# The last sums of a stage end quarter by quarter, and the last quarter is transposed between the two halves of the next stage's first weight unit

## The chip, the cores and the metric

The kernel runs on one core of a Trainium2 chip. The metric is the device time of one execution in microseconds, taken as the median of several runs. Five engines work side by side: TensorE (PE; its weight loads are PEld) multiplies and transposes, VectorE (DVE), ScalarE (ACT) and GpSimd (POOL) work element by element, and SyncE (SP) issues the loads and stores.

## What is computed

Two transformer blocks run over one sequence of 256 tokens with 1024 features. The first block has two layers; each adds a mixer to x (a short gated convolution in layer 0, windowed attention in layer 1) and then a PEER layer, in which every token chooses 16 of 16384 experts in each of 8 heads. The second block adds one mixed layer (pooling, mLSTM and blockwise attention side by side) and a gated feed-forward network (FFN). Ahead of every one of these x is normalised:

```python
def _rmsnorm(x, g):
    xf = x.astype(jnp.float32)
    y = xf * lax.rsqrt(jnp.mean(xf * xf, axis=-1, keepdims=True) + RMS_EPS)
    return (y * g.astype(jnp.float32)).astype(x.dtype)
...
    for i in range(DEPTH):
        j = i // N_MIXERS
        if i % N_MIXERS == 0:
            x = x + _short_conv_mixer(_rmsnorm(x, conv_norm_g[j]), conv_w_in[j], conv_w[j], conv_w_out[j])
        else:
            x = x + _windowed_gqa(_rmsnorm(x, attn_norm_g[j]), attn_w_qkv[j], attn_sink[j],
                                  attn_w_o[j], rel_bias)
        x = x + _peer(_rmsnorm(x, ffn_norm_g[i]), peer_w_q[i], peer_subkeys[i], peer_u[i], peer_v[i])
    return _rmsnorm(x, final_norm_g)
```

## The kernel before

All products are made in float32 precision out of three products of halves: a number is split into a high half (a copy to a shorter float) and a low half (what is left), and high x high, high x low and low x high are summed. Weights stream in as units of 128 x 1024. For each unit SyncE loads it into one of four `raw` buffers, ScalarE casts the high half `wh` (L127) into one of three buffers, and VectorE or POOL makes the low half `wl` (L128). `lo_on["pat"]` says which of the two: "P" is POOL, "V" is VectorE. `pump_split` does this up to a unit, `prepare` up to three units ahead of use. The loads that it issues wait for a `raw` buffer, that is, for the low half of the unit four places back.

Two kinds of products use a unit. `c_unit` (weights stand, 24 products of 256 columns, 8 column groups k) gives an output with tokens along the columns. `t_mm` (tokens stand, 12 products of 512 columns) gives an output with tokens along the partitions. The sums at the end of a stage are of the second kind. They fill four PSUM banks 4 to 7, one for each token half b and 512 columns n; such a sum is called a quarter (b, n) here.

At the end of a stage `t_end` takes the last two units together and closes the quarters in turn. `arrive` adds a quarter to x on VectorE (`add_x`, L243 or L245) and transposes its four column groups of x on TensorE (L269) into PSUM, two groups to a bank (`spot`). Then `settle` brings the transposed x, times the gain g, to the two halves that the next stage multiplies with: ScalarE copies a group (L278), VectorE makes its low half (L279). After the first token half it splits one more weight unit, with POOL. The row scales of the norm are not in it: `norm_scales` works them out beside the first unit (sums of squares on ScalarE, a short chain on VectorE), and `spread` lays them along the columns with an identity times the scale (L328), a product with ones (L329) and a copy to `rbc` (L330).

This happens at five places: conv to peer 0 (about 98 to 111 us), peer 0 to attention (927), attention to peer 1 (1031), peer 1 to block 2 (1860; here with `low=True`, where both token halves of a group share a bank, and the first units are of the kind `t_mm`), and block 2's mixer to the FFN (1999). A sixth `t_end` closes the kernel with the stores of the result.

The order on TensorE and SyncE is that of the program text. On ScalarE, VectorE and POOL a scheduler sets a fixed order when the kernel is built: an instruction goes when its inputs are there, the earlier one in the text first. `behind(st["after"])` puts an instruction behind a given one on its engine; `settle` sets it to its last copy, so that the casts and the sums of squares traced later queue behind that.

In `peer`, SyncE loads the subkeys (L421) and stores x to `x_d` (L423) after `settle`; the first scores (L429) need the subkeys. `rescale` (L562 to L565), `top16` and the choice of experts run on VectorE beside the units; the transposes L502 to L504 take what they give.

Of the kernel before, what the change touches and what calls it, by code (L numbers as in the profile page):

```python
# [40 lines left out]
def kernel(ctx: ExitStack, tc: tile.TileContext, a, out):  # L41
# [122 lines left out]

    def t_half(o, h, l, sh, sl, b, n, first, last):
# [38 lines left out]
    def t_end(k, n, get, cur, arrive):  # L204
# [15 lines left out]
        for nn in range(2):  # L220
            arrive(0, nn)
            part(1, nn, 0)
        for nn in range(2):
            part(1, nn, 1)
        for nn in range(2):
            arrive(1, nn)

    def t_phase(n, get, cur, arrive, during=None, k0=0, root=True):
        if root:
            table("sqrt_and_others")  # L230
        pat, lo_on["pat"] = lo_on["pat"], "V"
        t_run(k0, n - 2, n, get, cur, during)
        t_end(n - 2, n, get, cur, arrive)
        lo_on["pat"] = pat
# [30 lines left out]
    def landing(scale=None, low=False):  # L265
        def arrive(b, n):
            add_x(b, n, scale)
            for c in range(4 * n, 4 * n + 4):
                T.transpose(spot(b, c, low), x[:, b, c * 128:c * 128 + 128], ident)  # L269
        return arrive  # L270

    def settle(g, low=False, dst=None):

        h, l = dst or (xh, xl)
        for b in range(2):
            bs = slice(b * 128, b * 128 + 128)
            for c in range(8):
# [3 lines left out]
            if b == 0:  # L281
# [3 lines left out]
        st["after"] = i  # L285
# [39 lines left out]
    def spread(bk, off=0):  # L325

        for b in range(2):
            V.tensor_scalar(gt[b][:, :128], ident, col(b, 5, off), None, op0=ALU.mult)  # L328
            T.matmul(bk[:, b * 128:b * 128 + 128], ones, gt[b][:, :128], start=True, stop=True)  # L329
# [67 lines left out]
    t_phase(8, lambda k: split_small(G[k]), first, landing(), root=False)  # L397


    def peer(layer):  # L400
        xq = renew(F32R)
        xq = [xq[:, 8 * i:8 * i + 8] for i in range(2)]
        settle(cols[:, C_FFNG + 8 * layer:C_FFNG + 8 * layer + 8], dst=xq)
# [174 lines left out]
        lo_on["pat"] = "P"  # L578
        st["ready"] = 0
        for hp in range(18):  # L580
            if hp < 16:
# [3 lines left out]
                c_unit(bank[hp % 3][:, :256], src=xq)  # L585
                if hp == 0:
                    norm_scales()
# [50 lines left out]
        t_phase(128, lambda k: split_small(slot(k)), cur, landing(1.0 / WSCALE, layer == 1), during)  # L638
# [12 lines left out]
    def attention():  # L651
# [11 lines left out]
        settle(cols[:, C_ATTNG:C_ATTNG + 8])  # L663
        lo_on["pat"] = "P"
        for i in range(2):
            c_unit(bank[i][:, :256])
            if i == 0:
                norm_scales()
# [103 lines left out]
        t_phase(8, lambda k: split_small(ao[k]), cur, landing(), None, 4)  # L772
# [21 lines left out]
    def block2():  # L794
        sg = ar(64, 2).rearrange("p (b n) -> p b n", b=2)
        settle(g2, low=True)

        for k in range(8):
# [3 lines left out]
            if k == 0:  # L802
                norm_scales_final(gbc)
# [499 lines left out]
```

## Time and profile before

| | us |
|---|---|
| three runs | 2204.69, 2203.78, 2201.51 |
| median | 2203.78 |
| the profiled execution, its own time | 2201.73 |
| its span, first to last instruction | 2200.0 |

| engine | busy, share of the span |
|---|---|
| TensorE, products and transposes | 97% |
| TensorE, weight loads | 88% |
| VectorE | 76% |
| ScalarE | 52% |
| POOL | 19% |

A busy share is a mean over stages that have different limits. The profile's page gives it for the whole execution; the timeline lists the instructions in order of time with the wait ahead of each and the engine and line that ended it; the windows give the busy time by stretch. A group of equal instructions that follow each other stands in one row with its count; its time is from the first's start to the last's end.

### The profile page before, as it was taken

Reading aid. Unit: us, or ns where it says so; the run is one execution under the profiler, and the core shown is the slowest. Engines: PE = TensorE matmul, PEld = TensorE weight load, DVE = VectorE, ACT = ScalarE, POOL = GpSimd, SP = SyncE. Lnnn points to the kernel's source line nnn. Section 1 sums busy time; section 2 is a strip of 40 time slices with the busy share of each in tenths; the row PEclk is TensorE's granted clock in tenths of the full one; section 3 lists DMA queues with packets and bytes.
Section 4 is the critical chain, followed back from the end, with each engine's and each line's share of the span. In section 5 each row is a group of like instructions: output and inputs, shape, how many; then the busy total and the mean of one; then the engine's idle time right before and its main releaser. Section 6 shows DMA issues by size and latency. Waiting matters only on the chain.

```text
span 2200.0 us, 38262 instructions
## 1 busy us (share of the span) xinstructions
PE 2131.1 (97%) x14590; PEld 1943.2 (88%) x14590; DVE 1675.0 (76%) x3091; ACT 1145.7 (52%) x2102; POOL 409.1 (19%) x176
## 2 busy tenths in 40 slices
PE   9999799999999999998997999999999999889999
PEld 9899799999988888886997999999888888768998
DVE  7799968897566666676999688965666666797998
ACT  4455345554555555566553455545555555655443
POOL 0068630000000000053686300000000001550000
PEclk9999899999999999999998999999999999999999
DMA  7586454445667666633554554456676665434564
GB/s 230 173 238 192 138 176 155 154 155 173 202 194 238 208 192 193 190 116 98 181 168 134 175 157 154 154 173 203 194 223 193 192 193 180 146 94 143 184 189 145
DMA packets 109024, 384.44 MB, mean 175 GB/s; under 512 B 11876, under 2 KB 15332, under 8 KB 108584
## 3 DMA queue, kind: packets, MB, share of 16 engines
q1 hardware_dynamic: 108552, 381.81, 56.1%
q8 instruction: 114, 1.87, 0.3%
q14 instruction: 70, 0.57, 0.1%
q10 hardware_dynamic: 288, 0.19, 0.0%
HBM read 374.61 MB, written 7.34 MB: 174 GB/s over the span
## 4 chain that ended last, share of the span: by engine, by line
PE 88%; DVE 5%; issue 3%; POOL 2%; ACT 1%; DMA 1%; POOLq 0%; SPq 0%; ACTq 0%
PE bank L159 15%; PE bank L161 15%; PE bank L160 15%; PE bank L177 12%; PE bank L178 12%; PE bank L181 12%; PE bank L532 3%; POOL wl L128 2%; DVE arena L857 1%; ACT wh L127 1%; PE bank L429 0%; DMA x_d<-x 0%; PE bank L735 0%; DVE x L243 0%; DVE wl L128 0%
## 5 line engine op out<-in xcount | busy, mean ns | idle before, releaser
L127 ACT ACTIVATE wh<-raw 128x1024 fp32r<-128x1024 f32 x691 | 732.3, 1060 | 466.3 <-PE bank L160 226.9
L128 DVE TENSOR_TENSOR wl<-raw,wh 128x1024 fp32r<-128x1024 f32 x537 | 659.1, 1227 | 256.0 <-ACT wh L127 255.3
L159 PE MATMUL bank<-xh,wh 128*128 128x256 f32 x2792 | 808.9, 290 | 19.0 <-ACT arena L553 11.3
L161 PE MATMUL bank<-xh,wl 128*128 128x256 f32 x2792 | 795.2, 285 | 2.0 <-POOL wl L128 1.4
L160 PE MATMUL bank<-xl,wh 128*128 128x256 f32 x2792 | 794.8, 285 | 0.0
L128 POOL TENSOR_TENSOR wl<-raw,wh 128x1024 fp32r<-128x1024 f32 x154 | 390.4, 2547 | 959.7 <-ACT wh L127 957.7
L159 PEld LDWEIGHTS bank<-xh,wh 128*128 128x128 f32 x2792 | 539.8, 193 | 24.9 <-ACT arena L553 12.1
L161 PEld LDWEIGHTS bank<-xh,wl 128*128 128x128 f32 x2792 | 539.4, 193 | 4.5 <-POOL wl L128 3.2
L160 PEld LDWEIGHTS bank<-xl,wh 128*128 128x128 f32 x2792 | 540.2, 193 | 1.5 <-DVE xl L279 0.8
L177 PE MATMUL bank<-wh,ah 128*128 128x512 f32 x1160 | 454.6, 392 | 0.0
L178 PE MATMUL bank<-wl,ah 128*128 128x512 f32 x1160 | 453.2, 391 | 0.0
L181 PE MATMUL bank<-wh,al 128*128 128x512 f32 x1160 | 358.1, 390 | 0.0
L186 ACT ACTIVATE ah<-arena 128x256 fp32r<-128x256 f32 x270 | 112.3, 416 | 286.9 <-PE bank L178 279.2
L177 PEld LDWEIGHTS bank<-wh,ah 128*128 128x128 f32 x1160 | 218.8, 189 | 47.1 <-issue 2.1
L181 PEld LDWEIGHTS bank<-wh,al 128*128 128x128 f32 x1160 | 218.5, 188 | 45.9
L178 PEld LDWEIGHTS bank<-wl,ah 128*128 128x128 f32 x1160 | 218.8, 189 | 44.5
L187 DVE TENSOR_TENSOR al<-arena,ah 128x256 fp32r<-128x256 f32 x270 | 114.7, 425 | 118.9 <-PE bank L181 109.5
L523 DVE TENSOR_TENSOR x<-iota,ijT 128x1024 f16<-128x1024 f16 x128 | 89.9, 704 | 53.0 <-PE bank L532 53.0
L310 POOL TENSOR_TENSOR top<-x,arena 128x512 f32<-128x512 f32 x4 | 5.1, 1288 | 631.9 <-DVE x L245 631.9
L546 ACT ACTIVATE arena<-bank 128x284 f32<-128x284 f32 (+42 forms) x128 | 38.8, 303 | 131.0 <-DVE arena L544 131.0
L525 DVE TENSOR_TENSOR x<-x,wT 128x1024 f16<-128x1024 f16 x128 | 96.2, 753 | 0.0
L532 PE MATMUL bank<-x 128*128 128x128 f16 x1024 | 81.2, 220 | 0.0
(296 smaller groups left out, 1978.9 us busy)
## 6 DMA issues: line engine op xcount, KB each, us to landing
raw<-in_u_dram SPq DMA_DIRECT2D x256, 512.0 KB, 3.5
raw<-in_v_dram SPq DMA_DIRECT2D x256, 512.0 KB, 3.6
raw<-in_ff_dram SPq DMA_DIRECT2D x66, 512.0 KB, 3.5
raw<-in_wq_dram SPq DMA_DIRECT2D x32, 512.0 KB, 3.6
raw<-in_conv_in_dram SPq DMA_DIRECT2D x23, 512.0 KB, 3.8
raw<-in_conv_out_dram SPq DMA_DIRECT2D x8, 512.0 KB, 3.5
f_d<-arena SPq DMA_DIRECT2D x8, 512.0 KB, 7.1
raw<-in_aq_dram SPq DMA_DIRECT2D x8, 512.0 KB, 3.8
```

The costliest lines, as they stand in the source:

```text
L127: S.activation(h, r, AF.Copy)
L128: (P if pat[lo_on["i"] % len(pat)] == "P" else V).tensor_sub(l, r, h)
L159: T.matmul(out_ps, hv[:, k], ah[:, k], start=k == 0, stop=False)
L160: T.matmul(out_ps, hv[:, k], al[:, k], start=False, stop=False)
L161: T.matmul(out_ps, lv[:, k], ah[:, k], start=False, stop=k == 7)
L177: T.matmul(bank[4 + b * 2 + n], sh[:, bs], h[:, ns], start=first, stop=False)
L178: T.matmul(bank[4 + b * 2 + n], sh[:, bs], l[:, ns], start=False, stop=False)
L181: T.matmul(bank[4 + b * 2 + n], sl[:, bs], h[:, ns], start=False, stop=last)
L186: S.activation(h, src, AF.Copy)
L187: V.tensor_sub(l, src, h)
L525: V.tensor_tensor(W, E[:, 1:2].to_broadcast(shape), wT[:, c, :, :, None, :].to_broadcast(shape), op=ALU.mult)
L532: T.matmul(bk[:, t * 128:t * 128 + 128], E[:, 0, t // 2, :, t % 2], W[:, q, t // 2, :, t % 2], start=q == 0, stop=q == 1)
```

## The change

`t_end` gets two functions in place of `arrive`: `add` adds a quarter to x, `turn` transposes it. The last sums are reordered so that quarter (1,0) is closed before quarter (1,1), and each quarter is added when it is closed. Quarter (0,0) is transposed ahead of token half 1 as before, (0,1) after quarter (1,0) is closed, (1,0) before the last three products. The transposes of (1,1) are kept in `st["turn"]`.

`settle` goes by quarters and takes `first`: it calls `first(0)` after quarter (1,0), then transposes quarter (1,1), copies it, and calls `first(1)`. In four stages `first` is `c_halves`, the first unit in two halves of 12 products with column groups 0 to 3 and 4 to 7; `prepare` runs in its second half. In block 2 `first` is a whole unit each time. `norm_scales` follows `settle`. `spread` makes the two identities times scales with one product on VectorE and one product with ones of 256 columns.

```diff
@@ -162,6 +162,23 @@
         if ahead:
             prepare()
 
+    def c_halves(out_ps, src=None):
+
+        u = []
+
+        def half(i):
+            if not i:
+                u.extend(unit())
+            ah, al = src or (xh, xl)
+            hv, lv = [w.rearrange("p (k m) -> p k m", k=8) for w in u]
+            for k in range(4 * i, 4 * i + 4):
+                T.matmul(out_ps, hv[:, k], ah[:, k], start=k == 0, stop=False)
+                T.matmul(out_ps, hv[:, k], al[:, k], start=False, stop=False)
+                T.matmul(out_ps, lv[:, k], ah[:, k], start=False, stop=k == 7)
+            if i:
+                prepare()
+        return half
+
     def t_half(o, h, l, sh, sl, b, n, first, last):
         bs = slice(b * 128, b * 128 + 128)
         ns = slice(n * 512, n * 512 + 512)
@@ -201,7 +218,7 @@
             if during:
                 during(k)
 
-    def t_end(k, n, get, cur, arrive):
+    def t_end(k, n, get, cur, add, turn=lambda b, n: None):
 
         pat, lo_on["pat"] = lo_on["pat"], "P"
         prepare()
@@ -217,20 +234,24 @@
         for nn in range(2):
             part(0, nn, 0)
             part(0, nn, 1)
-        for nn in range(2):
-            arrive(0, nn)
-            part(1, nn, 0)
-        for nn in range(2):
-            part(1, nn, 1)
-        for nn in range(2):
-            arrive(1, nn)
-
-    def t_phase(n, get, cur, arrive, during=None, k0=0, root=True):
+            add(0, nn)
+        turn(0, 0)
+        part(1, 0, 0)
+        part(1, 0, 1)
+        add(1, 0)
+        turn(0, 1)
+        part(1, 1, 0)
+        turn(1, 0)
+        part(1, 1, 1)
+        add(1, 1)
+        st["turn"] = turn
+
+    def t_phase(n, get, cur, add, turn, during=None, k0=0, root=True):
         if root:
             table("sqrt_and_others")
         pat, lo_on["pat"] = lo_on["pat"], "V"
         t_run(k0, n - 2, n, get, cur, during)
-        t_end(n - 2, n, get, cur, arrive)
+        t_end(n - 2, n, get, cur, add, turn)
         lo_on["pat"] = pat
 
     def sumsq(b, n, src=None, off=0):
@@ -263,26 +284,37 @@
         return bank[i][:, o:o + 128]
 
     def landing(scale=None, low=False):
-        def arrive(b, n):
+        def add(b, n):
             add_x(b, n, scale)
+
+        def turn(b, n):
             for c in range(4 * n, 4 * n + 4):
                 T.transpose(spot(b, c, low), x[:, b, c * 128:c * 128 + 128], ident)
-        return arrive
-
-    def settle(g, low=False, dst=None):
+        return add, turn
+
+    def settle(g, first, low=False, dst=None):
+
 
         h, l = dst or (xh, xl)
-        for b in range(2):
+
+        def quarter(b, n):
             bs = slice(b * 128, b * 128 + 128)
-            for c in range(8):
+            for c in range(4 * n, 4 * n + 4):
                 i = S.activation(h[:, c, bs], spot(b, c, low), AF.Copy, scale=g[:, c:c + 1])
                 V.scalar_tensor_tensor(l[:, c, bs], spot(b, c, low), g[:, c:c + 1], h[:, c, bs],
                                        op0=ALU.mult, op1=ALU.subtract)
-            if b == 0:
+            return i
+
+        for b, n in ((0, 0), (0, 1), (1, 0)):
+            quarter(b, n)
+            if (b, n) == (0, 1):
                 pat, lo_on["pat"] = lo_on["pat"], "P"
                 pump_split(st["use"] + 2)
                 lo_on["pat"] = pat
-        st["after"] = i
+        first(0)
+        st["turn"](1, 1)
+        st["after"] = quarter(1, 1)
+        first(1)
 
     def root(b, off=0):
 
@@ -324,9 +356,9 @@
 
     def spread(bk, off=0):
 
-        for b in range(2):
-            V.tensor_scalar(gt[b][:, :128], ident, col(b, 5, off), None, op0=ALU.mult)
-            T.matmul(bk[:, b * 128:b * 128 + 128], ones, gt[b][:, :128], start=True, stop=True)
+        V.tensor_tensor(gt[0].rearrange("p (b t) -> p b t", b=2), ident[:, None, :].to_broadcast([128, 2, 128]),
+                        sm[:, off + 5:off + 14:8, None].to_broadcast([128, 2, 128]), op=ALU.mult)
+        T.matmul(bk[:, :256], ones, gt[0], start=True, stop=True)
         V.tensor_copy(rbc, bk[:, :256])
 
     def rsqrt_small(dst, v, t):
...
-    t_phase(8, lambda k: split_small(G[k]), first, landing(), root=False)
+    t_phase(8, lambda k: split_small(G[k]), first, *landing(), root=False)
...
-        settle(cols[:, C_FFNG + 8 * layer:C_FFNG + 8 * layer + 8], dst=xq)
+        lo_on["pat"] = "P"
+        settle(cols[:, C_FFNG + 8 * layer:C_FFNG + 8 * layer + 8], c_halves(bank[0][:, :256], xq), dst=xq)
...
-                c_unit(bank[hp % 3][:, :256], src=xq)
-                if hp == 0:
+                if hp:
+                    c_unit(bank[hp % 3][:, :256], src=xq)
+                else:
                     norm_scales()
...
-        settle(cols[:, C_ATTNG:C_ATTNG + 8])
         lo_on["pat"] = "P"
-        for i in range(2):
-            c_unit(bank[i][:, :256])
-            if i == 0:
-                norm_scales()
+        settle(cols[:, C_ATTNG:C_ATTNG + 8], c_halves(bank[0][:, :256]))
+        norm_scales()
+        c_unit(bank[1][:, :256])
...
-        settle(g2, low=True)
-
-        for k in range(8):
+
+        def tm(k):
             h, l = unit()
             t_mm(h, l, xh[:, k], xl[:, k], k == 0, k == 7)
             prepare()
-            if k == 0:
-                norm_scales_final(gbc)
+
+        settle(g2, tm, low=True)
+        norm_scales_final(gbc)
+        for k in range(2, 8):
+            tm(k)
...
-        settle(cols[:, C_LN2:C_LN2 + 8])
+        settle(cols[:, C_LN2:C_LN2 + 8], c_halves(bank[0][:, :256]))
+        norm_scales()
...
-                c_unit(bank[(c % 2) * 2 + s][:, :256])
-                if (c, s) == (0, 0):
-                    norm_scales()
+                if c or s:
+                    c_unit(bank[(c % 2) * 2 + s][:, :256])
```

## Rows read from the trace of the kernel before

**Rows 1.** The page's first part: busy us, share of the span, instructions.

```profile
PE 2131.1 (97%) x14590; PEld 1943.2 (88%) x14590; DVE 1675.0 (76%) x3091; ACT 1145.7 (52%) x2102; POOL 409.1 (19%) x176
```

**Rows 2.** Timeline of TensorE, first place: start us, us, instruction, count, [wait <-releaser].

```profile
101.70 0.66 PE L269 MATMUL bank<-ident,x 128*128 128x128 f32 x4 [0.29 <-DVE x L243]
102.11 0.47 PE L168 MATMUL bank<-wh,ah 128*128 128x512 f32 x1
...
103.24 0.48 PE L168 MATMUL bank<-wh,ah 128*128 128x512 f32 x1
...
105.16 0.39 PE L170 MATMUL bank<-wh,al 128*128 128x512 f32 x1
...
108.48 0.28 PE L159 MATMUL bank<-top,wh 128*128 128x256 f32 x1
...
116.40 0.39 PE L329 MATMUL bank<-gt,ones 128*128 128x128 f32 x2
117.33 0.49 PE L329 MATMUL bank<-gt,ones 128*128 128x128 f32 x2 [0.54 <-DMA x_d<-x]
```

**Rows 3.** Timeline of VectorE, first place.

```profile
99.82 1.23 DVE L128 TENSOR_TENSOR wl<-raw,wh 128x1024 fp32r<-128x1024 f32 x1 [1.49 <-ACT wh L127]
100.96 1.28 DVE L243 TENSOR_TENSOR x<-bank,x 128x512 f32<-128x512 f32 x2
...
103.36 1.21 DVE L279 SCALAR_TENSOR_TENSOR top<-bank,cols,top 128x128 fp32r<-128x128 f32 x4 [0.18 <-ACT top L278]
...
115.87 1.40 DVE L328 TENSOR_SCALAR gt<-ident,sm 128x128 f32<-128x128 f32 x1
117.19 0.41 DVE L562 TENSOR_TENSOR gt<-top 128x256 f32<-128x256 f32 x1
...
118.19 2.14 DVE L562 TENSOR_TENSOR gt<-top 128x256 f32<-128x256 f32 x1
```

**Rows 4.** Busy time by stretch, peer stage 0: stretch, us, each engine's busy us (instructions).

```profile
118.00:237.00 119.00, 109.44 (x904) 107.94 (x902) 118.81 (x417) 56.00 (x93) 83.79 (x33) 0.99 0.69 192
```

**Rows 5.** Waits of TensorE: us in total, times, longest.

```profile
PE bank L503 <- DVE arena L499: 13.5, 2, 6.7
```

**Rows 6.** Timeline of ScalarE, first place.

```profile
102.17 0.62 ACT L278 ACTIVATE top<-bank,cols 128x128 fp32r<-128x128 f32 x2 [2.39 <-PE bank L269]
102.96 1.22 ACT L278 ACTIVATE top<-bank,cols 128x128 fp32r<-128x128 f32 x4 [0.16 <-DVE top L279]
104.27 1.06 ACT L127 ACTIVATE wh<-raw 128x1024 fp32r<-128x1024 f32 x1
...
106.13 2.33 ACT L278 ACTIVATE top<-bank,cols 128x128 fp32r<-128x128 f32 x8 [0.29 <-PE bank L269]
```

**Rows 7.** Timeline of POOL, first place.

```profile
117.67 2.39 POOL L128 TENSOR_TENSOR wl<-raw,wh 128x1024 fp32r<-128x1024 f32 x1 [0.48 <-ACT wh L127]
```

**Rows 8.** Timeline of ScalarE, start of block 2.

```profile
1867.17 4.42 ACT L278 ACTIVATE xh<-bank,sm 128x128 fp32r<-128x128 f32 x16 [0.86 <-PE bank L269]
```

**Rows 9.** Timeline of TensorE, start of block 2.

```profile
1867.79 0.47 PE L177 MATMUL bank<-wh,xh 128*128 128x512 f32 x1
...
1871.05 0.39 PE L177 MATMUL bank<-wh,xh 128*128 128x512 f32 x1
...
1875.06 0.50 PE L178 MATMUL bank<-wl,xh 128*128 128x512 f32 x1 [0.91 <-POOL wl L128]
```

**Rows 10.** Timeline of SyncE, first place.

```profile
108.24 0.43 SPq L421 DMA_DIRECT2D arena<-in_sk_dram  x1
...
111.93 2.71 SPq L102 DMA_DIRECT2D raw<-in_wq_dram  x2
```

**Rows 11.** DMA issues: transfer, queue, count, KB each, median us to landing.

```profile
arena<-in_sk_dram SPq DMA_DIRECT2D x2, 1024.0 KB, 7.3
```

**Rows 12.** Busy time by stretch within the mixer of block 2.

```profile
1960.70:1964.70 4.00, 1.19 (x8) 0.68 (x6) 4.00 (x8) 0.38 (x1) 2.35 (x1) 1.00 0.26 45
1964.80:1968.20 3.40, 3.23 (x14) 2.85 (x15) 3.40 (x9) 2.36 (x6) 0.00 (x0) 0.50 0.31 127
```

More of the change, by code (lines that the diff above doesn't have):

```diff
@@ L576, in advance @@
                     run["live"] = False
-        lo_on["pat"] = "P"
         st["ready"] = 0
@@ L636, in during @@
                 load_b2()
-        t_phase(128, lambda k: split_small(slot(k)), cur, landing(1.0 / WSCALE, layer == 1), during)
+        t_phase(128, lambda k: split_small(slot(k)), cur, *landing(1.0 / WSCALE, layer == 1), during)
         lo_on["pat"] = "VP"
@@ L771, in attention @@
                 values(step - 4, bank[6 + step % 2] if step < 8 else bank[2 + step % 2])
-        t_phase(8, lambda k: split_small(ao[k]), cur, landing(), None, 4)
+        t_phase(8, lambda k: split_small(ao[k]), cur, *landing(), None, 4)
     tok = ar(0, 8).rearrange("p (b n) -> p b n", b=2)
@@ L1118, in block2 @@
         fetch(7)
-        t_end(6, 8, None, cur, landing())
+        t_end(6, 8, None, cur, *landing())
         lo_on["pat"] = "V"
-        settle(cols[:, C_LN2:C_LN2 + 8])
+        settle(cols[:, C_LN2:C_LN2 + 8], c_halves(bank[0][:, :256]))
+        norm_scales()
         upb = [ar(2 * i, 2)[:, 0:258] for i in range(4)]
```

## The prediction, written before the changed kernel had run

> **What bounds the kernel now.** I read the page's first part, then the timeline of TensorE, VectorE, ScalarE and SyncE around the end of one stage, then the busy time by stretch and the waits of TensorE. TensorE is busy for 97% of the span [rows 1], so only its waits can be won, and the change works on those at the five places where a stage ends and the next one starts from a normalised x. I call the sum of one token half b over 512 columns n a quarter (b, n).
>
> At the first place [rows 2] the order of TensorE is: four transposes of quarter (0,0) at 101.70 (they wait for the addition to x), three products at 102.11, four transposes, nine products from 103.24 to the one at 105.16, eight transposes, the first weight unit. In the run of nine a product takes (105.16 - 103.24) / 8 = 0.24 us; four transposes take 102.11 - 101.70 = 0.41. The seventh product of the unit starts at 108.48, and from there to 116.40 lie 66 products, 0.12 each. So the unit ends at 108.48 + 18 x 0.12 = 110.64. Without a wait it would end at 105.40 (the nine products) + 0.82 (eight transposes) + 24 x 0.12 = 109.10. **1.54 us are lost there** while ScalarE and VectorE bring x into its two halves (L278, L279). Another 0.4 is lost ahead of 101.70: the addition (100.96) stands behind a VectorE split that began at 99.82 [rows 3]. The change moves neither, so that part stays.
>
> The two peer stages are bound otherwise: from 118 to 237 us VectorE is busy 118.81 of 119 us [rows 4], and TensorE then waits up to 6.7 us for it, once in each [rows 5]. There, what counts is when VectorE's long run begins, which is after the scales are spread (L330).
>
> **Part 1: quarters end one by one, the last is transposed amid the next unit.** Three quarters are transposed before the last three products, the fourth between the two halves of the unit. No product or transpose is added; the same work without waits ends at about 109.1 as before. What decides is how fast one quarter alone is brought in. Rows show it for quarter (0,0): transposes at 101.70, two copies from 102.17 [rows 6], and the third copy only at 102.96, when VectorE has read the first group of that bank; its low half runs from 103.36 [rows 3] to 103.71. ScalarE and VectorE take turns on a bank of two groups. So from the first transpose the products of the first group may start at 0.90 and 1.28, those of the second at 1.68 and 2.06 (a copy's 0.37 and a low half's 0.35, 0.05 for the signal). With all four banks of a token half open, as now, the turns overlap; with one quarter there are two banks.
> The Trainium skill, page "PSUM — Partial Sum Buffer", section "PSUM bank collisions raise a hardware error", has the rule behind it: guard PSUM by bank, not by address, since two engines must not touch one bank at once. It speaks against small quarters; the trace agrees (the third copy waits 0.16 us for VectorE), and without it the first wait below would be 0.8 instead of 1.17.
>
> Second half of the unit: wanted 0.41 after its first transpose, it waits 0.49 + 0.26 + 0.16 + 0.26 = 1.17 us at its first five products. Nothing covers this: TensorE runs in order.
> First half: TensorE comes to its transposes at 104.68 (101.70 + 0.41 + six products + 0.41 + three products), ends the last three products at 105.81 and then wants the unit. Alone, the same turns would cost 0.5 to 0.8. But ScalarE has a cast of weights to do (L127, 1.06 us), which starts when the three products that last read its buffer are done (104.27 now, 104.87 then), and which stood ahead of two copies of the older token half: two and four copies precede it, eight belong to b = 1, sixteen are all [rows 6]. If that order holds: cast to 105.83, two copies to 106.35, first copy to 106.72, product at 106.77 (0.96 late); VectorE has the last addition (0.64, half of the two at 100.96 [rows 3]) and two low halves first, so the low half is there at 107.46 (0.63 late); the second group adds 0.16 + 0.26. Together 2.01.
> Sum: 2.01 + 1.17 - 1.54 = **+1.6 us for one place**; with the cast behind the copies 0.78 + 1.17 - 1.54 = +0.4. I take +1.6, the order that the rows show, and keep +0.4 to +2.
>
> Attention and the last stage (FFN) are paced by TensorE here and take this whole: **+1.6 each**. Queued behind the last copy are the casts of the next units: cast 1.06 and POOL's low half 2.4 [rows 6, 7] end 3.5 after it, and its third product comes some 4 us after: covered by about half a microsecond.
>
> **Part 2: the start of block 2** has whole 512-column units of 12 products, of which the first needs one column group. Before, the copies wait until 1867.17 and run in one piece [rows 8], the first unit takes 1871.05 - 1867.79 = 3.26 instead of 12 x 0.24 = 2.88, and the third waits 0.91 for POOL's low half [rows 9]. At most 0.4 + 0.91 and the wait ahead of the first unit can go, some 1.6; but a group of b = 1 follows two groups of b = 0 in the same bank, and a cast may fill the gap. I take -0.8, bounds -1.6 and +0.3.
>
> **Part 3: the spread by one product.** Two VectorE products of a column (L328) and four TensorE passes become one tensor_tensor and passes of the same columns: TensorE unchanged. L328 took 1.40 where POOL was at work; a tensor_tensor of the new shape (L562) took 0.41 alone and 2.14 beside POOL: it started at 118.19 while POOL's instruction ran from 117.67 to 120.06, and ended just behind it [rows 3, 7]. The Trainium skill, "SBUF — State Buffer", section "Who interferes with whom", says that a tensor_tensor with both inputs in SBUF contends with GpSimd's reads and the second to issue blocks. By it the scales come at 120.7 below if POOL is first and at 118.96 if not; these rows show both.
> The scales follow the last copy. That copy ends at 108.46 now (106.13 + 2.33 [rows 6]) and at 109.26 + 1.88 = 111.14 then; 7.4 later comes the product with the identity: 118.55, and 118.96 to 120.7 when it is done (up to 1.4 earlier, as one L328 less stands in the chain). TensorE arrives at 116.40 + 1.64 = 118.04. Now it waits 0.54 and goes on at 117.33 [rows 2]; then at 118.04 to 120.7. So the long run of VectorE in a peer stage starts 0.7 to 3.4 later. In FFN the same loss of lead costs 0 to 1.0; I take +0.4. Conv and attention: about 0.
>
> **Part 4: SyncE.** In the peer stages the unit's prepare() now comes before the load of the subkeys (L421). Now this is issued at 108.24, ahead of two weight loads at 111.93 and, done by 114.64, a second [rows 10], which wait for POOL to free their buffers. Then it stands behind both: 114.64 (111.93 + 2.71) + 1.64 = 116.3 or later, and 7.3 us to land [rows 11]: 123.6 at the earliest. The first scores (just behind the spread's 117.33 now) then wait some 3 to 5 us on TensorE. TensorE has the 6.7 us of [rows 5] in hand; VectorE has the rescaling to do meanwhile. Bounds for a peer stage: 0 (all absorbed) to +5 (VectorE starves). I take **+2.0 each**, nearest to the middle of the spread's delay.
>
> **Sum**: 1.6 + 1.6 + 0.4 + 2 x 2.0 - 0.8 = +6.8 us. The final stage gains nothing: its last addition follows its last product in either order. The profiled run took 2201.73 (span 2200.0), 2.05 below the median of the three, so 2208.5 on its scale and **2210.5** as a median.
>
> **Rivals.** (a) The cast falls behind the copies, and only the turns on a bank remain: 0.4 + 0.4 + 2 x 0.5 - 0.8 = +1.0, 2204.8. For it: the cast becomes ready (104.87) only 0.3 before the first copy of quarter (1,0) could start (104.68 + 0.47); against: the order now. (b) Faster: each half is covered as meant. If a quarter's second group came 0.4 us sooner (the point from which the turns cost nothing) and the cast went elsewhere, a place would lose 0.8 instead of 1.54; attention and FFN -0.7 each, peers -1.5 each (with the 0.54 and the settle), block 2 -1.6: -6.0, 2197.8. Against: [rows 3, 6]. (c) The late subkeys starve VectorE: peers +5 each, 2216.5; for it, VectorE has no gap to give back [rows 4]. (d) TensorE's clock: a stretch of 4 us with TensorE busy 1.19 was followed by 3.4 us at a granted 0.50, 1.2 instead of 2.4 GHz [rows 12]. Waits of 3 us in 6 might do the same, 1.7 us at each of two places: 2214. That nothing changes is in (a).
>
> **How the numbers follow.** Forecast 0.50 (own range 2205.5 to 2214.5), (a) 0.24, (b) 0.08, (c) 0.12, (d) 0.06. About 0.2%, 4.4 us, is what a measurement can tell from no change; 0.06 of the forecast and nearly all of (a) lie within it. Slower 0.62, same 0.30, faster 0.08. The range reaches down into (a) and up over (c): 2203 to 2218.
>
> **What would show it.** Right: a wait of the second half's first product for L278 at four of the five places; the first half waiting for a copy behind L127; L429 waiting for the subkeys' DMA; a shorter wait at L503; the third unit of block 2 not waiting for POOL. Wrong: copies of (1,0) ahead of L127 on ScalarE, or L503 reached no later than before.

## The result, and the profile after

The changed kernel takes 2216.34 us in the median (2215.35 to 2217.74), the kernel before 2203.92 (a fourth run counted in): 12.4 us slower, a ratio of 1.0061 (95% interval 1.0049 to 1.0073). The forecast was 2210.5 with a range of 2203 to 2218: right in direction and range, but the loss is nearly twice the 6.7 us forecast. The forecast's own range ended at 2214.5; the time is that of rival (c), 2216.5, which had a chance of 0.12. The profiled execution has a span of 2213.5 us, 13.5 above that of before. The profiled execution of e3_one_product below took 4208.54 us, nearly twice its other eleven; its ratio leaves it out, and no row is read from it.

The first part of the page of the kernel after: the span, then busy us, share and instructions of each engine. Against [rows 1] TensorE's busy time is the same within 0.2%, in a longer span; VectorE is busy 26.8 us less, and a reason for most of that comes below.

```profile
span 2213.5 us, 38223 instructions
PE 2135.1 (96%) x14578; PEld 1947.1 (88%) x14578; DVE 1648.2 (74%) x3085; ACT 1148.5 (52%) x2102; POOL 407.7 (18%) x176
```

To place the loss I took, from the timeline of TensorE, the start of the first transposes of x at each of the five places (101.70 and 102.28 at the first), and so the length of each stage from place to place:

| stage, from place to place | before | after | more | forecast |
|---|---|---|---|---|
| up to the first place (conv) | 101.70 | 102.28 | +0.58 | about 0 |
| first peer stage | 828.96 | 832.84 | +3.88 | +2.0 |
| attention | 103.30 | 103.59 | +0.29 | +1.6 |
| second peer stage | 828.77 | 834.15 | +5.38 | +2.0 |
| block 2 | 139.79 | 140.58 | +0.79 | -0.8 |
| FFN to the end | 197.44 | 200.10 | +2.66 | +2.0 |

The last row hardly varies between kernels of one form (197.44 to 197.49 in six kernels with the old end of a stage). The peer stages vary by a microsecond or so, block 2 by more (139.29 to 142.09 in five kernels with the old form there), and so does conv: its row shifted by -0.8 to +3.6 between the kernels below, for reasons that they don't settle.

**The first place after**, TensorE's timeline (start us, us, instruction, count, [wait and releaser]; answers to [rows 2]):

```profile
102.28 0.66 PE L292 MATMUL bank<-ident,x 128*128 128x128 f32 x4 [0.29 <-DVE x L264]
...
106.20 0.40 PE L187 MATMUL bank<-wh,al 128*128 128x512 f32 x1
106.91 0.38 PE L175 MATMUL bank<-top,wh 128*128 128x256 f32 x1 [0.32 <-ACT top L303]
107.63 0.39 PE L176 MATMUL bank<-top,wh 128*128 128x256 f32 x1 [0.34 <-DVE top L304]
...
108.67 0.38 PE L176 MATMUL bank<-top,wh 128*128 128x256 f32 x1 [0.25 <-DVE top L304]
...
109.72 0.60 PE L292 MATMUL bank<-ident,x 128*128 128x128 f32 x4
110.56 0.38 PE L175 MATMUL bank<-top,wh 128*128 128x256 f32 x1 [0.24 <-ACT top L303]
...
112.79 0.28 PE L159 MATMUL bank<-top,wh 128*128 128x256 f32 x1
```

The first half could start at 106.43 (106.20 and a product's 0.23) and gives way to the transposes at 109.72: 3.29 us for 12 products of 0.12, **1.85 lost**. The second half could start at 109.72 + 0.41 and ends at 112.79: 2.66, **1.22 lost**. The second unit starts 10.51 us after the first transposes; before it was 110.64 - 101.70 = 8.94. That is 1.57 us more, and the same row gives 1.59, 1.56 and 1.58 at the other three places with two halves.

ScalarE at the same place (answers to [rows 6]): the cast L127 stands behind the first two copies of the second quarter, ahead of its other two and of the third quarter's four (the six at 106.51), and the last quarter's four copies come in two pairs.

```profile
105.55 1.06 ACT L127 ACTIVATE wh<-raw 128x1024 fp32r<-128x1024 f32 x1 [0.34 <-ACT top L303]
106.51 1.98 ACT L303 ACTIVATE top<-bank,cols 128x128 fp32r<-128x128 f32 x6
110.14 0.62 ACT L303 ACTIVATE top<-bank,cols 128x128 fp32r<-128x128 f32 x2 [1.64 <-PE bank L292]
110.92 0.63 ACT L303 ACTIVATE top<-bank,cols 128x128 fp32r<-128x128 f32 x2 [0.16 <-DVE top L304]
```

**The peer stages after.** Waits of TensorE over the whole kernel (us in total, times, longest; answers to [rows 5]; L536 is L503 of before, L462 the first scores, L361 the spread's pass):

```profile
PE bank L536 <- DVE arena L532: 12.6, 2, 6.3
PE bank L159 <- ACT arena L586: 11.3, 2, 5.6
PE bank L462 <- DMA arena<-in_sk_dram: 10.0, 2, 5.3
...
PE bank L361 <- DVE gt L359: 3.9, 4, 1.3
```

SyncE (answers to [rows 10]): four weight loads instead of two, and behind them, at 117.76 instead of 108.24, the subkeys.

```profile
101.66 16.05 SPq L102 DMA_DIRECT2D raw<-in_wq_dram  x4
117.76 0.43 SPq L454 DMA_DIRECT2D arena<-in_sk_dram  x1
118.24 0.94 SPq L456 DMA_DIRECT2D x_d<-x  x2
```

Busy time by stretch (stretch, us, busy us and instructions of PE, PEld, DVE, ACT, POOL, then the granted clock, DMA share and GB/s): in both peer stages TensorE is granted half its clock (1.2 instead of 2.4 GHz) in and behind the wait for the subkeys. The kernel before has 1.00 in the first of these stretches.

```profile
122.30:129.10 6.80, 3.04 (x14) 3.08 (x15) 6.36 (x19) 2.26 (x6) 0.00 (x0) 0.50 0.99 351
1057.60:1067.70 10.10, 5.92 (x28) 5.95 (x29) 8.50 (x22) 2.26 (x6) 1.25 (x1) 0.50 0.79 278
```

The scales are there when VectorE copies them from the spread, before and after:

```profile
117.85 0.42 DVE L330 COPY rbc<-bank 128x256 f32<-128x256 f32 x1 [0.25 <-PE bank L329]
```

```profile
120.76 0.42 DVE L362 COPY rbc<-bank 128x256 f32<-128x256 f32 x1 [0.79 <-PE bank L361]
```

VectorE from the spread's end to the second Exp of the search, by lines (busy us, mean ns, idle before and its releaser), after:

```profile
L475 DVE MAX8 arena<-arena 128x8 f32<-128x128 f32 x32 | 7.6, 279 | 11.1 <-ACT arena L466 11.1
...
L595 DVE TENSOR_TENSOR gt<-top 128x256 f32<-128x256 f32 x7 | 3.6, 551 | 0.0
L598 DVE TENSOR_TENSOR xl<-gt,xh 128x256 fp32r<-128x256 f32 x8 | 3.5, 464 | 0.4
L596 DVE TENSOR_TENSOR gt<-gt,rbc 128x256 f32<-128x256 f32 x8 | 3.0, 415 | 0.0
```

and the same three lines of the rescaling in the kernel before:

```profile
L565 DVE TENSOR_TENSOR xl<-gt,xh 128x256 fp32r<-128x256 f32 x8 | 9.7, 1221 | 0.2 <-ACT xh L564 0.2
L562 DVE TENSOR_TENSOR gt<-top 128x256 f32<-128x256 f32 x8 | 6.4, 805 | 0.0
L563 DVE TENSOR_TENSOR gt<-gt,rbc 128x256 f32<-128x256 f32 x8 | 5.3, 685 | 0.0
```

VectorE now runs dry for 11.1 us because the scores come late, and most of that comes back: the rescaling takes 10.7 us instead of 21.4 (the 10.1 above and an eighth addition of 0.59 that ran ahead of the spread). With TensorE standing, no weights are cast and POOL has no low half to make: it is idle for 9.9 us from 122.16 (0.00 busy in the stretch from 122.30, 4.85 before). The Trainium skill, "SBUF — State Buffer", section "Who interferes with whom", has a DVE instruction with two SBUF inputs contend with a GpSimd instruction that reads SBUF. The traces agree: a subtraction of L565 or L598 took 0.40 to 0.43 us where POOL was idle or nearly so, and 1.68 to 2.36 where it worked through most of it; the means of 1221 and 464 ns come of four such long ones before and none after (one of 0.78). What is left per stage, from the copy of the scales (117.85 before, 120.76 after) to the second Exp (240.54, 245.26): 122.68 us before, 124.50 after, so 1.8 us; 2.4 in the second peer stage.

### The profile page after: what moved, and what is told of

Same layout as the page of the kernel before. It is cut to its first block, busy times and chain, and to the rows that moved or that the text cites. A ratio compares the mean times of both kernels' runs of the same rounds, so it can differ in the third digit from the quotient of the medians.

```text
span 2213.5 us, 38223 instructions
## 1 busy us (share of the span) xinstructions
PE 2135.1 (96%) x14578; PEld 1947.1 (88%) x14578; DVE 1648.2 (74%) x3085; ACT 1148.5 (52%) x2102; POOL 407.7 (18%) x176
## 4 chain that ended last, share of the span: by engine, by line
PE 91%; DVE 4%; issue 2%; ACT 1%; DMA 1%; POOL 0%; SPq 0%; POOLq 0%; ACTq 0%
PE bank L159 16%; PE bank L161 16%; PE bank L160 16%; PE bank L194 12%; PE bank L195 12%; PE bank L198 12%; PE bank L565 3%; PE bank L462 1%; DMA arena<-in_sk_dram 1%; ACT wh L127 1%; POOL wl L128 0%; PE bank L292 0%; PE bank L766 0%; DVE wl L128 0%; PE bank L176 0%
## 5 line engine op out<-in xcount | busy, mean ns | idle before, releaser
L127 ACT ACTIVATE wh<-raw 128x1024 fp32r<-128x1024 f32 x691 | 732.5, 1060 | 488.4 <-PE bank L160 227.6
L159 PE MATMUL bank<-xh,wh 128*128 128x256 f32 x2776 | 805.1, 290 | 17.2 <-ACT arena L586 11.3
L565 PE MATMUL bank<-x 128*128 128x128 f16 x1024 | 81.2, 220 | 0.0
```

Of the source, the lines that this page charges most:

```text
L127: S.activation(h, r, AF.Copy)
L159: T.matmul(out_ps, hv[:, k], ah[:, k], start=k == 0, stop=False)
L565: T.matmul(bk[:, t * 128:t * 128 + 128], E[:, 0, t // 2, :, t % 2], W[:, q, t // 2, :, t % 2], start=q == 0, stop=q == 1)
```

## Experiments

Times are medians; ratios are to the kernel before, run on the same chip, with 95% intervals.

### The subkeys ahead again, or late alone

e1_sk_first, on the changed kernel: the first unit's prepare() comes behind the peer stage's own loads.

```diff
-            if i:
+            if i and ahead:
                 prepare()
...
         nc.sync.dma_start(skT, a["sk"][layer])
         for b in range(2):
             nc.sync.dma_start(x_d[b], x[:, b])
+        prepare()
```

> The changed kernel, except that in both peer stages the loads of the subkeys and the stores of x_d are issued ahead of the first unit's prepare(), as before. Theory (late subkeys): in the changed kernel the subkeys were issued at 117.76 instead of 108.24, TensorE waited 5.3 and 4.7 us for them, its clock was then granted at 0.5 for 6.83 and 10.24 us, and VectorE ran dry; the two peer stages lost 3.5 and 5.4 us. With the load ahead, that wait is gone, no half-clock stretch stands at 122 or 1057, VectorE has work from 121.1 on without a gap, and only the later scales (121.10 against 118.19) remain: some 2.3 us for each peer stage, 4.3 us less than the changed kernel: 2212 us. Rival (the later scales set the time, the subkeys are hidden behind them): the wait goes, but the time stays at 2216, within 1 us.

Measured: 2210.91 us, ratio 1.0034 (1.0022 to 1.0046): 5.4 us less than the changed kernel. The wait at L462 is gone, and the clock is at its upper level in both places:

```profile
117.00:130.00 13.00, 11.69 (x97) 11.43 (x96) 10.00 (x25) 8.32 (x18) 9.14 (x5) 1.00 0.87 275
1054.00:1068.00 14.00, 13.18 (x109) 13.13 (x110) 13.05 (x31) 6.74 (x14) 7.73 (x4) 1.00 0.53 169
```

The scales are as late as in the changed kernel: their copy comes 18.48 us after the first transposes, 16.15 before. The rival, that the scales alone set the time, falls. But the theory's 2.3 us for each peer stage isn't what the trace shows: the stages are 0.69 and 2.87 us longer than before. With the same delay of the scales, the second Exp of the search stands 0.47 us further behind the first transposes than before in the first stage and 2.80 in the second, so the price of late scales differs between the stages, and this run doesn't show why.

e2_late_sk, on the kernel before: those loads alone, behind the first unit.

```diff
                 c_unit(bank[hp % 3][:, :256], src=xq)
                 if hp == 0:
+                    load_sk()
                     norm_scales()
```

> The kernel before, with one part of the change alone: the loads of the subkeys and the stores of x_d are issued behind the first unit's prepare(). Theory (late subkeys): issued at some 116, landed at some 123, TensorE waits about 5 us for them in each peer stage, its clock falls there, and VectorE is short of scores: 3 us (2 to 4) for each peer stage, 2208 to 2212 us. Rival (the 6.7 us for which TensorE waits at L503 anyway absorb it): 2204, within 1 us, with a wait at L503 that is shorter by as much as the new one is long.

Measured: 2206.76 us, ratio 1.0016 (1.0007 to 1.0025), 3.3 us more. The subkeys were issued at 114.51, and these waits of TensorE and VectorE stand in both stages (L505 is L503 of before):

```profile
PE bank L505 <- DVE arena L501: 12.6, 2, 6.3
PE bank L431 <- DMA arena<-in_sk_dram: 8.1, 2, 4.1
```

```profile
DVE arena L444 <- ACT arena L435: 19.1, 12, 1.9
```

A slower kernel, below the theory's 4 to 8 and above the rival's 2204. The rival's mechanism falls: the wait at L505 is 6.3 us instead of 6.7, not shorter by the new 4.1. In this profiled execution the peer stages were 2.15 and 0.30 longer; most of the rest of its +5 is block 2, which the edit doesn't touch and where TensorE had half its clock for 20 us instead of 14. Late subkeys thus cost 3.3 us alone in the medians, of which the trace has 2.45 in the peer stages, and 5.4 on top of the rest of the change, where they are issued later still (15.5 us after the first transposes, 13.0 here).

### The spread

e3_one_product: before, with the new spread alone.

```diff
-        for b in range(2):
-            V.tensor_scalar(gt[b][:, :128], ident, col(b, 5, off), None, op0=ALU.mult)
-            T.matmul(bk[:, b * 128:b * 128 + 128], ones, gt[b][:, :128], start=True, stop=True)
+        V.tensor_tensor(gt[0].rearrange("p (b t) -> p b t", b=2), ident[:, None, :].to_broadcast([128, 2, 128]),
+                        sm[:, off + 5:off + 14:8, None].to_broadcast([128, 2, 128]), op=ALU.mult)
+        T.matmul(bk[:, :256], ones, gt[0], start=True, stop=True)
```

> The kernel before, with the one product for the spread alone. Theory: the product of both columns comes after both roots; in the conv stage that costs 0.6 us as it did in the changed kernel (there TensorE waited 0.42 for it), in the FFN nothing (TensorE is not early there without the quarters), in the peer stages the chain to the scales is shorter by one L328 of 1.25 us, so rbc is there up to 1.2 us earlier unless POOL holds the new product up: 2202 to 2205 us. Rival (POOL's lock makes the new product cost 2 us where it stands): rbc about 2 us later in each peer stage, 2207 to 2209 us.

Measured: 2202.63 us, ratio 1.0000 (0.9991 to 1.0009). No difference. e4_two_products is the changed kernel with that edit the other way round.

> The changed kernel with the old spread (two products of a column, four passes on TensorE). Theory (the one product comes later than the first of two, and stands where TensorE has no lead left): in the changed kernel TensorE waited for it 0.42 us in the conv stage, 1.31 us in the first peer stage and 0.86 us in the FFN. With the old form the pass of the second column still waits for the same chain of roots, so only what the wider product itself takes is won: 0.4 us in conv, up to 0.5 in FFN, up to 1 in each peer stage: 2213.5 to 2215.5 us. Rival (the delay is that of the last copy and of the sums of squares behind it, whatever the spread's form): 2216 within 1 us. Rival (the first of two products under POOL's lock was worth its time): 2 us slower, 2218.

Measured: 2214.72 us, ratio 1.0051 (1.0038 to 1.0065); 1.6 us below the changed kernel, within both intervals. VectorE at the first place of e4:

```profile
115.64 1.01 DVE L360 TENSOR_SCALAR gt<-ident,sm 128x128 f32<-128x128 f32 x1
...
119.54 1.93 DVE L360 TENSOR_SCALAR gt<-ident,sm 128x128 f32<-128x128 f32 x1
...
122.06 0.42 DVE L362 COPY rbc<-bank 128x256 f32<-128x256 f32 x1 [0.58 <-PE bank L361]
```

Beside POOL the two products make the scales come 20.56 us after the first transposes, against 18.48 with one, so with the quarters the one product is 2 us better at this place. But TensorE then waits longer for the scales (8.8 us in all instead of 3.9) and less for the subkeys (2.2 us at one place instead of 10.0 at two), and the sum moves little. The time lies in the theory's 2213.5 to 2215.5, but its account fails in the peer stages, where the scales come later and not earlier; in the FFN 0.33 us is won, as it said. The first rival's mechanism (scales late whatever the form) holds in part; the other's, the product beside POOL, holds for the rows and not for the time.

### The cast behind the third quarter

e5_cast_behind, on the changed kernel:

```diff
         for b, n in ((0, 0), (0, 1), (1, 0)):
-            quarter(b, n)
-            if (b, n) == (0, 1):
-                pat, lo_on["pat"] = lo_on["pat"], "P"
-                pump_split(st["use"] + 2)
-                lo_on["pat"] = pat
+            i = quarter(b, n)
+        st["after"] = i
+        pat, lo_on["pat"] = lo_on["pat"], "P"
+        pump_split(st["use"] + 2)
+        lo_on["pat"] = pat
```

> The changed kernel, except that the cast of the next unit's weights (L127) stands behind the copies of the third quarter on ScalarE instead of ahead of them. Theory (the cast ahead of the copies costs the first half its second): in the changed kernel the first half of the unit lasts 3.29 us where 12 products take 1.44, and ScalarE's cast ran from 105.55 to 106.5 ahead of the third quarter's copies. Behind them, the first half should wait 0.8 to 1.2 us less; attention and FFN take that whole, the peer stages in part: 2212.5 to 2214.5 us. Rival (the turns of ScalarE and VectorE on a bank set the pace, and VectorE's last addition stands in the chain): the first half is as long, 2216 within 1 us. Second rival: the cast comes too late for the second unit, TensorE waits there for POOL instead, and the time stays.

Measured: 2215.50 us, ratio 1.0057 (1.0044 to 1.0071); no difference in time to the changed kernel. ScalarE's copies of the third quarter now start at 106.30, 3.4 us after the first transposes (102.88) instead of 4.2, and the cast follows at 108.47:

```profile
106.30 1.40 ACT L303 ACTIVATE top<-bank,cols 128x128 fp32r<-128x128 f32 x5 [0.50 <-PE bank L292]
108.21 0.37 ACT L303 ACTIVATE top<-bank,cols 128x128 fp32r<-128x128 f32 x1 [0.50 <-DVE top L304]
108.47 1.05 ACT L127 ACTIVATE wh<-raw 128x1024 fp32r<-128x1024 f32 x1
```

TensorE's second unit starts 9.99 us after the first transposes, 10.51 with the cast ahead: 0.52 of the 0.8 to 1.2 expected. What remains is VectorE's (the last addition stands ahead of its low halves), and at block 2 the late cast is paid with a wait for POOL:

```profile
108.74 0.39 PE L176 MATMUL bank<-top,wh 128*128 128x256 f32 x1 [0.60 <-DVE top L304]
```

```profile
1881.01 0.50 PE L195 MATMUL bank<-wl,xh 128*128 128x512 f32 x1 [1.99 <-POOL wl L128]
```

So the theory holds at about half its size, 0.5 us won at four places, and the second rival at the fifth, where about 2 us are given back.

### Block 2 alone

e8_block2_only: the kernel before, with the new end of a stage at the start of block 2 only, where the first two units stand on either side of the last quarter's transposes.

> The kernel before, with the quarter-by-quarter end and the split first unit at the start of block 2 alone. Theory (as the trace of the changed kernel shows it): 84 products behind the stage's end, block 2 is 0.3 us ahead of the kernel before, no more, since the copies of the second token half's quarters wait in turn for VectorE; the whole time then 2203 to 2204 us, and what a run shows beyond that lies in the half-clock stretches inside the mixer. Rival (the prediction's -0.8 to -1.6): 2202 us.

Measured: 2202.68 us, ratio 0.9999 (0.9990 to 1.0008). From the first transposes of block 2 to those of the FFN it took 139.62 us, 139.79 before. About the theory's figure; the part of the change that I forecast to win wins 0.2 in the trace, and no difference in the medians.

### What TensorE's waits in the search are worth

e7_pause: before, and nothing of the change, with four units ahead of the transposes of the search's result.

```diff
+                yield 8.4
                 bk = bank[3]
                 T.transpose(bk[:, 0:128], ij[:, 0].rearrange("p h k -> p (h k)"), ident)
```

> The kernel before, with no part of the change; in the peer stages four more weight units go ahead of the transposes of the search's result on TensorE (one step of 8.4 in the hand-written order). It measures what the two waits of TensorE for VectorE (6.74 us at L503, 5.64 us behind ScalarE's L553) and the half-clock stretch of 13.65 us behind them are worth. Theory (TensorE is only ahead of VectorE there, and has other units to do): four units of 2.88 us cover both waits, the clock stays at its upper level, and each peer stage wins 8 to 11 us: 2182 to 2188 us. Rival (VectorE's own order moves with it, and the wait stands four units later): 2204 within 2 us.

Measured: 2205.43 us, ratio 1.0012 (1.0003 to 1.0021). The rival: the two waits of before, 6.74 for the search's result [rows 5] and 5.64 behind ScalarE, became one of 13.2, behind ScalarE, and ScalarE's row tells why. Before:

```profile
PE bank L159 <- ACT arena L553: 11.3, 2, 5.6
240.54 0.31 ACT L478 ACTIVATE arena<-arena 128x128 f32<-128x128 f32 x1 [16.22 <-DVE arena L477]
```

and in e7:

```profile
PE bank L159 <- ACT arena L554: 26.3, 2, 13.2
```

```profile
241.61 0.31 ACT L478 ACTIVATE arena<-arena 128x128 f32<-128x128 f32 x1 [16.21 <-DVE arena L477]
```

ScalarE has the second Exp of the search next in its order, waits 16.21 us for VectorE at it, and the evacuations that would free TensorE's banks (L554) stand behind. e9_after_pause is the same edit on the changed kernel.

> The changed kernel, with the same four units ahead of the transposes of the search's result in the peer stages. Theory (the change delays VectorE's long run, and the wait at L503 is where TensorE pays for it): with a spare lead TensorE doesn't pay for VectorE's lateness, so the change costs less here than without the pause: what stays is the 1.6 us at each end of a stage, the 5 us for the subkeys on TensorE itself with its half-clock stretch, and the FFN's 2.6, so 8 to 13 us above the kernel before with the pause. Rival (TensorE's own waits make up the whole loss and the wait at L503 is unconcerned): 12.4 us above, as without the pause.

Measured: 2216.89 us, ratio 1.0062 (1.0048 to 1.0076). 11.5 us above e7; with the wait only moved, it says nothing on the question.

e10_exp_later moves that Exp seven evacuations down ScalarE's order and keeps the four units ahead of the first of the two results only:

```diff
-                S.activation(wf[:, b], wf[:, b], AF.Exp)
+                with behind(evs[-9] if b else None):
+                    S.activation(wf[:, b], wf[:, b], AF.Exp)
...
+                if not b:
+                    yield 8.4
                 bk = bank[3]
...
-                S.activation(slot(j)[:, t:256], bk[:, t:256], AF.Gelu)
+                evs.append(S.activation(slot(j)[:, t:256], bk[:, t:256], AF.Gelu))
```

> The kernel before, with no part of the change. In the peer stages the second Exp of the search (L478) stands seven evacuations later in ScalarE's order, and four units go ahead of the first transposes. Theory (the run with the pause alone showed it: the wait only moved, since ScalarE stood 16.2 us at that Exp for VectorE while TensorE's banks waited behind it for L553): with both moved, TensorE neither waits 6.7 us at L503 nor 5.6 us behind L553, and the half-clock stretch of 13.65 us behind them goes; 8 to 11 us in each peer stage: 2182 to 2188 us. Rival (VectorE is the bound of this stretch whatever the order, and another instruction waits for it next): 2200 to 2206 us.

Measured: **2176.61 us, ratio 0.9876** (0.9860 to 0.9891), 27 us faster than before, more than expected. ScalarE waits 1.09 us at the Exp, and TensorE is busy without a gap at its upper clock in the stretch where the kernel before had 4.92 of 14 us at a mean of 0.51:

```profile
243.42 1.28 ACT L479 ACT_TABLE_LOAD   x1
245.80 0.31 ACT L479 ACTIVATE arena<-arena 128x128 f32<-128x128 f32 x1 [1.09 <-DVE arena L477]
```

```profile
234.00:248.00 14.00, 14.00 (x119) 14.00 (x118) 13.93 (x32) 8.23 (x12) 12.44 (x6) 1.00 0.69 199
```

The same stretch before:

```profile
234.00:248.00 14.00, 4.92 (x20) 4.24 (x21) 13.96 (x30) 5.36 (x8) 6.13 (x3) 0.51 0.14 40
```

The four units alone won nothing in e7; the later Exp alone was not run, so the 27 us belong to the two together.

e11_after_exp_later is the changed kernel with this edit.

> The changed kernel, with the same later Exp and four units. Theory (in the peer stages the change costs what it makes VectorE late, 2.3 us by the scales and 1.8 to 2.4 by the subkeys, because TensorE and ScalarE stand still for VectorE at this Exp): where nobody waits there, VectorE's lateness costs nothing, and of the change's 12.4 us there stay 1.6 + 1.3 + 5 us of TensorE's own waits in each peer stage at most, less than without the later Exp if the half-clock stretch behind the subkeys is paid once: 6 to 12 us above the kernel before with the later Exp. Rival (the loss in the peer stages is TensorE's own waiting at the scales and the subkeys): 14 to 20 us above that kernel, since nothing absorbs them any more.

Measured: 2187.95 us, ratio 0.9930 (0.9917 to 0.9944), 11.3 us above e10. At the upper end of the theory's 6 to 12. TensorE's own waits stay, as it said (waits of TensorE in e11 below), but the loss doesn't shrink: the peer stages are 4.20 and 5.74 us longer than in e10, against 3.88 and 5.38 without the later Exp. Where VectorE's lateness is out of the way, TensorE's own waits take its place:

```profile
PE bank L462 <- DMA arena<-in_sk_dram: 8.8, 2, 4.6
PE bank L361 <- DVE gt L359: 5.2, 4, 1.7
```

At the transposes of the first search result e11 is 3.92 us behind e10, and at the next place still 3.93. The loss in a peer stage is held twice, once by VectorE's chain and once by TensorE.

e12_exp_later_one_product is e10 with the one product of e3.

> The kernel before with the later Exp and four units, and with the one product for the spread. It shows in a trace what the one product does in the order of before: theory: in the conv stage the pass comes 0 to 0.6 us later, in the peer stages rbc comes 0.5 to 1.5 us earlier (one L328 of 1.25 us less ahead of the second root, which the sums of squares wait behind); the time is that of the later Exp alone within 2 us. Rival (the product stands under POOL's lock): rbc 2 us later, 2 to 4 us slower than the later Exp alone.

Measured: 2175.67 us, ratio 0.9869 (0.9854 to 0.9884), the same as e10. The product on VectorE and the copy of the scales:

```profile
117.57 1.59 DVE L327 TENSOR_TENSOR gt<-ident,sm 128x256 f32<-128x256 f32 x1
119.95 0.42 DVE L330 COPY rbc<-bank 128x256 f32<-128x256 f32 x1 [0.79 <-PE bank L329]
```

16.56 us after the first transposes (103.39), 16.15 before: 0.4 later, neither the 0.5 to 1.5 earlier of the theory nor the rival's 2 later.

## Why the prediction was right, and where its sizes were off

**The boundary itself (+1.6 a place) was right.** Measured +1.57, first half 1.85 (worked out as 2.01), second half 1.22 (1.17). The order of rows (cast ahead of the third quarter) was kept, as assumed. That a quarter alone pays for the turns of ScalarE and VectorE on a bank shows in the 0.16 us ahead of the second pair of copies, the same as in [rows 6]. One point fell: with the cast behind the copies (e5) only 0.5 goes, not 1.2, for VectorE's chain is nearly as late.

**Attention: the step was right, the stage gave it back.** The second unit starts 1.59 late there, but the stage is only 0.29 longer. Busy time by stretch, before and after:

```profile
965.00:1015.00 50.00, 41.66 (x287) 34.24 (x287) 43.80 (x111) 31.33 (x97) 14.27 (x6) 0.86 0.21 67
```

```profile
965.00:1015.00 50.00, 41.70 (x313) 35.17 (x311) 45.45 (x112) 31.06 (x91) 14.71 (x7) 0.90 0.26 79
```

The mean granted clock is 0.90 instead of 0.86: 0.10 / 0.5 x 50 = 10 us at half clock instead of 14, worth up to 2 us. Where the clock is nearly equal (0.91 in e10, 0.90 in e11, over the like stretches) the new form is 103.65 - 101.66 = 2.0 longer. The other traces agree: with about 10 us at half clock the old form takes 101.66 and 102.59 (e10, e12) and the new one 103.51 to 103.96 (six traces); with about 14 us the old form takes 103.31 to 103.81 (four traces). This is a comparison of runs, not an experiment on the clock, and why the new form has less time at half clock isn't shown.

**Block 2 (-0.8) was mis-sized.** The first 84 products end 0.3 earlier (22.79 us after the first transposes, 23.11 before), and e8 wins 0.2: the wait of 0.91 for POOL went, as named, and waits of 0.40 and 0.86 for the copies of the last quarters came. The rest of the stage then lost 1.1 with more time at half clock inside the mixer (0.85 over 1900 to 1935, 0.90 before), which I had not priced. This row moves by more than that between kernels of one form, so the 1.1 need not be the change's.

**FFN (+2.0) was +2.66**: the boundary 1.58 and the spread 1.1 instead of 0.4. Its pass waits 0.86 for the product there; I had given 0 to 1.0, and the chosen value was low.

**The peer stages carry the error: +2.0 forecast, +3.9 and +5.4 measured.** The step that failed is "TensorE has the 6.7 us of [rows 5] in hand", with +2.0 "nearest to the middle of the spread's delay". The delay of the scales was right: 18.48 - 16.15 = 2.33, in a range of 0.7 to 3.4. The subkeys' time was right as well (issue forecast at 116.3 or later, seen at 117.76; a wait of 3 to 5, seen 5.3 and 4.7). But I let TensorE's later wait absorb them, so the sum held nothing for them. That wait was no reserve. L536 and L586 still wait 6.3 and 5.6 us, only later: ScalarE stands at an Exp for VectorE, TensorE for ScalarE, and so what has made VectorE late by then arrives at TensorE. The second Exp comes 4.72 us later (245.26, 240.54; 0.58 of them from conv), the next place 4.47. e7 and e10 show this chain, e1 the share of the subkeys (5.4 us of the 12.4). What the later scales cost by themselves stays open: with the subkeys early (e1) the peer stages are 0.69 and 2.87 us longer.

**Rival (c) was nearer, and (d) was there too.** (c) had +5 for a peer stage, 3 more than the forecast; by e1 the late subkeys cost 5.4 us, 2.7 a stage. They did starve VectorE as it says, for 11.1 us in a stage, but in the trace of the change that left only 1.8 to 2.4, as the rescaling won back some 11 us beside an idle POOL: a term that no part of my working had. That the whole time comes within 0.2 us of (c)'s 2216.5 is luck: attention came out 1.3 below its term and block 2 1.6 above, in (c) as in the forecast. The clock of (d) fell at both predicted waits, for 6.8 and 10.1 us. I take it for no cost of its own on top here, since VectorE's chain sets the end of the search anyway, and for one in e11; no run tests that.

**Signs.** The wait of the second half's first product for L303 (0.24), the first half's wait for a copy behind L127 (0.32), and L462's for the DMA all stand in the trace. A shorter wait at L503 was there (6.3 for 6.74), but read as absorption it misled: the one behind L586 stayed.

The conv stage's +0.58 isn't explained: the pass of the spread waited 0.42 there, but the same row shifts by more between kernels of one form.

## What to carry to other kernels

A wait on the critical engine is slack for a delay only if what it waits for doesn't get later by the same delay: follow the chain behind the releaser before you book it. When a helper now calls the "fetch ahead" earlier, look at what else shares that DMA queue, here a load that two weight loads overtook. On an engine whose order is fixed, an instruction that waits for a slow producer holds up what stands behind it, here the evacuations behind an Exp. Moving that Exp, with four units put ahead of the search's result, was worth 27 us, against 12 lost by everything in the change.

## What the runs showed of the hardware that was not expected

An engine that runs dry can get time back: VectorE's rescaling fell from 21.4 to 10.7 us when POOL was idle, so that 11 us of idling cost 2. And the clock's price goes beyond the wait: behind the subkeys' wait of 5.3 us TensorE stayed at 0.50 to 129.1, 3 us into its work. In e10 the 12.4 us of waits in a peer stage and the 13.5 us at 0.50 that stood with them went (a wait of 1.6 came elsewhere), and the stages became 13.5 and 13.3 us shorter: in the first TensorE is idle 11.0 us less, and busy 2.5 us less. It had worked for 4.7 of the 13.5 us at half clock, which is an estimated 2.4 lost.
